# Rewritten order of work in the input stage of a decoder block: passes grouped by part, one product moved between plain halves, squares, diagonals and rotary tables moved

## The chip, the cores and the metric

The kernel runs on one core of one Trainium2 chip. The metric is the device time of one execution in microseconds. Everything is in fp32 at the borders; the kernel is a single program in which most engines' instructions stand in the order in which the program writes them.

## What is computed

One decoder block for 1024 tokens with 1024 features, all fp32:

```python
h = rms_norm(x, mix_norm_g)
z_a, q, k, v, gate_logits = split(h @ w_in)           # z_a = (u, v) of the gMLP, 2 x 768
# A: chunks of 128 tokens, 4 channel groups, causal weights w_spatial
u, v = split(gelu(z_a));  v = rms_norm(v, gmlp_norm_g)
mixed = einsum('gts,bcsgd->bctgd', tril(w_spatial), v_chunks) + b_spatial
y_a = u * mixed
# B: dilated sliding-window attention, 12 heads of 64, rotary on the first quarter
q, k = partial_rope(q, positions), partial_rope(k, positions)
y_b = dilated_mixture_attention(q, k, v)
merged = sigmoid(g_A) * (y_a @ w_branch_a) + sigmoid(g_B) * (y_b @ w_branch_b)
x = x + merged @ w_out
h2 = rms_norm(x, ffn_norm_g)
a, val = split(h2 @ w_up)                             # 2 x 2816
x = x + (gelu(causal_dwconv3(a)) * val) @ w_down
return rms_norm(x, final_norm_g)
```

## The kernel before

**How a product is made.** Each fp32 operand of a large product is split into two parts, a high part (the value rounded to the short form `fp32r`) and a low part (the rest). A product is then three passes of matmuls: high weight by high left, high weight by low left, low weight by high left. `PASSES` lists them as pairs (w, a): w is the part of the weight, which is loaded into TensorE and stays, and a the part of the left side, which streams through. ScalarE (ACT) makes every high part by a copy, VectorE (DVE) every low part by subtracting that copy. For weights that is lines 165 and 166 (`to_parts`), for the left quarters lines 405, 406, 411 and 412 (`in_left`; where the part is wanted negated the copy scales by -1).

**The two ways of the input projection.** The columns of `w_in` are worked through in pairs n of two blocks of 128. Pairs 0 and 1, the first 512 columns of v, are plain products (`plain_op`, `plain_step`, `plain_final`): each covers two halves h of 512 tokens and two blocks i, with 8 k-tiles and so 24 matmuls of 128x512 for each (n, h, i). Their left side is x times the gain alone (`raw_left`), and the factor of the RMS norm comes in later, so TensorE can work before the norm is known. From pair 2 (`FIRST`) on, each pair takes the seven products of Strassen's scheme in Winograd's form, in the order P1, P2, P6, P7, P5, P4, P3 for pair 2 and P1, P6, P2, P7, P5, P4, P3 behind it. Each is a call of `in_product` and has 4 k-tiles, so 12 matmuls of 128x512. Their left sides are quarters of the normed x or sums of quarters (`LEFT`): P1 takes A11, P2 A12, P6 S2, P7 S3, P5 S1, P4 A22, P3 S4. P2, P4 and P3 add into the PSUM banks of P1, P7 and P5 (`SHARED`). After a product, ACT or DVE takes its bank: P1's is copied by ACT (line 530), P6, P7, P5, P4 and P3 are added by DVE into the result (line 537 is P7's), and for the gMLP's columns ACT then runs gelu.

**From the plain pairs to the normed x.** `beginning()` writes this order out. `square_row` (line 366) squares rows of x on ACT with a sum, four for each half; `load_rows` fetches the rows. `root` (GpSimd, POOL) makes the inverse root. `diagonal` (lines 383 and 385) puts the factors on four 128x128 diagonals, for half 0 on DVE and for half 1 on ACT. `spread` (line 391) multiplies them by a matrix of ones on TensorE, and `scale_x` (line 456) multiplies x by gain and spread factor on DVE, in place, one call for each k-tile. `x_sum` and `x_sum_dma` (line 474, an accumulating DMA of POOL's queue) form the sums of quarters, `parts_of` the two parts of each quarter. `in_load` fetches a weight block on SP's queue, and `in_ahead(i, far, look)` loads weight blocks up to `far` products ahead and makes the parts of those up to `look` ahead.

**What sets the order.** From the start up to product number `ORDERED` = 6 of the Strassen list (P3 of pair 2), DVE and ACT execute in exactly the written order (a manual schedule); behind that a scheduler places DVE's and ACT's work. TensorE's matmuls run in the written order throughout. `meanwhile(i)` is called after the i-th product and writes the preparations of later ones: S3 after P1, S1 after P2, A22 after P6, S4 after P7. Each product gives two ticks of a clock, one after each six matmuls, and `after(t, fn)` runs `fn` t ticks later. By these ticks `turn_v` (line 623) transposes blocks of v, with ACT taking the bank by a gelu into V (line 628); `norm_v` squares a row block of V (ACT, line 192), takes the root and scales (DVE, line 640); `spatial` (lines 652 and 660, bank `pm`) multiplies it by the causal weights, with DVE taking the bank. `turn_v`, `spatial`, `spread` and the rotary transposes share the two PSUM banks with the tag `tr`.

**The rotary tables.** `rot_tables` returns three lists: some 40 small steps of DVE and ACT that lead to the sines, sixteen widening copies on ACT (line 2238), and four turns, each of four transposes on TensorE (line 2255) and a copy by ACT (line 2256). `some(n)` writes the next n steps. Before, what is left of the steps and all widening copies come at `i == 6`, and all four turns at `i == 8`.

**The up stage.** Near 800 us the products with `w_up` begin (`beginning_up`). `up_product` is built like `in_product`, with its banks taken by DVE, and `up_ahead(load, op)` loads weight blocks and makes their high parts, up to those two numbers. Here DVE's low parts are not written at once: they go to a list, and `low(n)` writes the next n of them. `first_taps` is the first part of a convolution, four DVE operations.

## Time and profile before

| | |
|---|---|
| median of 3 runs | 1389.06 us (1388.65 to 1392.38) |
| profiled execution, its time | 1391.06 us |
| profiled execution, its span in the trace | 1389.1 us |
| mean granted TensorE clock in it | 0.996 |
| instructions in the span | 19247 |
| HBM traffic | 167.77 MB read, 64.29 MB written, 167 GB/s over the span |

The profile is one execution as the hardware profiler recorded it. A page gives for each engine (PE is TensorE's matmuls, PEld its weight loads, DVE VectorE, ACT ScalarE, POOL GpSimd, SP SyncE) its busy time and its share of the span. Views of the trace list waits (an engine, its line, what it waited for, the total, the number and the largest), a timeline of one engine (start, length, line, instruction, output<-inputs, sizes, count; in brackets the idle time before it and what ended it), and stretches of time with the busy time of each engine and the clock that was granted to TensorE. All times are in us from the span's start. The median of the runs lies 2.00 below the profiled execution's time.

### The profile page before, as it was taken

The numbers are of one execution on the slowest core, as the hardware profiler recorded it, in microseconds if no ns is written. First come the engines' busy times: TensorE is split into PE (matmuls) and PEld (weight loads), VectorE is DVE, ScalarE is ACT, GpSimd is POOL, SyncE is SP. The second block draws the span as 40 slices with busy tenths as digits, with TensorE's granted clock in tenths as the row PEclk, the third lists the DMA queues.
The fourth block names the chain that finished last, engine by engine and source line by source line (L and its number), as shares of the span: only waits on it lengthen the run. The fifth ranks groups of instructions, "written<-read, shape, count | busy, mean of one in ns | idle before, by whom it ended". The sixth has DMA issues, their size and how long they took to land.

```text
span 1389.1 us, 19247 instructions
## 1 busy us (share of the span) xinstructions
PE 1364.6 (98%) x6434; PEld 1130.7 (81%) x6434; DVE 1030.6 (74%) x1880; ACT 655.1 (47%) x1289; POOL 298.1 (21%) x295
## 2 busy tenths in 40 slices
PE   9889999999999999999999999999999999999997
PEld 7767888888888888888788878888888888888886
DVE  7868677686877987867889887766766667676674
ACT  7583355555544333634646444333433335455443
POOL 0111000000221000120001146655566553000003
PEclk9999999999999999999999999999999999999999
DMA  9424535354435997694843133333323327986563
GB/s 352 89 65 130 167 109 169 115 167 134 130 116 193 329 307 256 216 300 140 287 133 104 39 117 103 106 107 113 107 103 110 122 84 254 385 322 221 196 206 122
DMA packets 143875, 237.01 MB, mean 171 GB/s; under 512 B 13728, under 2 KB 57504, under 8 KB 143776
## 3 DMA queue, kind: packets, MB, share of 16 engines
q1 hardware_dynamic: 141248, 231.53, 49.5%
q0 software_dynamic: 1088, 2.10, 0.9%
q10 hardware_dynamic: 1440, 2.16, 0.4%
q8 instruction: 51, 0.84, 0.2%
q14 instruction: 48, 0.39, 0.1%
HBM read 167.77 MB, written 64.29 MB: 167 GB/s over the span
## 4 chain that ended last, share of the span: by engine, by line
PE 85%; DVE 6%; ACT 3%; issue 2%; POOL 2%; DMA 2%; SPq 0%; POOLq 0%; ACTq 0%; DVEq 0%
PE in_P L510 25%; PE uP L1788 19%; PE dn L2046 13%; PE up L1788 8%; PE pa L1260 5%; PE wo_P L1621 4%; PE pl L571 2%; PE pu L1767 2%; PE pb L1260 1%; PE pu L851 1%; DMA ld<-scr 1%; PE pp L835 1%; DVE G L166 1%; PE pm L660 1%; POOL st L903 1%
## 5 line engine op out<-in xcount | busy, mean ns | idle before, releaser
L510 PE MATMUL in_P<-R,G 128*128 128x512 f32 x1008 | 243.8, 394 | 1.8 <-ACT C L530 1.8
L510 PEld LDWEIGHTS in_P<-R,G 128*128 128x128 f32 x1008 | 185.4, 188 | 38.5 <-ACT C L530 2.2
L2046 PE MATMUL dn<-R 128*128 128x512 f32 x924 | 209.6, 389 | 0.0
L2046 PEld LDWEIGHTS dn<-R 128*128 128x128 f32 x924 | 173.4, 188 | 36.0
L165 ACT ACTIVATE G<-wr 128x512 fp32r<-128x512 f32 x126 | 79.1, 630 | 150.4 <-PE in_P L510 114.4
L165 ACT ACTIVATE R<-up 128x512 fp32r<-128x512 f32 x130 | 78.8, 627 | 125.1 <-DVE up L278 40.9
L510 PE MATMUL in_P<-G,G 128*128 128x512 f32 x504 | 124.1, 397 | 2.3 <-DVE C L537 2.3
L1788 PE MATMUL up<-G,R 128*128 128x512 f32 x504 | 121.4, 391 | 1.7 <-DVE R L166 1.7
L1788 PE MATMUL uP<-G,R 128*128 128x512 f32 x504 | 121.2, 389 | 0.0
L1788 PE MATMUL uP<-R 128*128 128x512 f32 x504 | 121.1, 389 | 0.0
L1788 PEld LDWEIGHTS up<-G,R 128*128 128x128 f32 x504 | 94.5, 188 | 22.7 <-DVE R L166 2.2
L510 PEld LDWEIGHTS in_P<-G,G 128*128 128x128 f32 x504 | 93.7, 190 | 21.1 <-ACT G L405 2.5
L1788 PEld LDWEIGHTS uP<-G,R 128*128 128x128 f32 x504 | 94.5, 188 | 19.8 <-issue 0.2
L1788 PEld LDWEIGHTS uP<-R 128*128 128x128 f32 x504 | 94.6, 188 | 19.6
L166 DVE TENSOR_TENSOR G<-wr,G 128x512 fp32r<-128x512 f32 x126 | 87.9, 699 | 24.2 <-ACT G L165 24.0
L166 POOL TENSOR_TENSOR R<-up,R 128x512 fp32r<-128x512 f32 x55 | 84.0, 1527 | 74.5 <-ACT R L165 74.5
L166 DVE TENSOR_TENSOR R<-up,R 128x512 fp32r<-128x512 f32 x75 | 63.0, 841 | 16.1 <-ACT R L165 15.9
L165 ACT ACTIVATE R<-db 128x512 fp32r<-128x512 f32 x77 | 48.1, 626 | 56.3 <-PE dn L2046 45.3
L166 DVE TENSOR_TENSOR R<-db,R 128x512 fp32r<-128x512 f32 x77 | 53.7, 701 | 25.8 <-ACT R L165 25.7
L1260 PE MATMUL pa<-R,G 128*128 128x512 f32 x288 | 67.9, 389 | 0.0
L1260 PEld LDWEIGHTS pa<-R,G 128*128 128x128 f32 x288 | 54.1, 188 | 11.2
L510 PE MATMUL in_P<-G 128*128 128x512 f32 x252 | 62.2, 393 | 0.0
(279 smaller groups left out, 2396.5 us busy)
## 6 DMA issues: line engine op xcount, KB each, us to landing
wr<-in_w_in_dram SPq DMA_DIRECT2D x45, 512.0 KB, 4.1
up<-in_w_up_dram SPq DMA_DIRECT2D x44, 512.0 KB, 3.5
dA<-gd SPq DMA_DIRECT2D x55, 256.0 KB, 5.1
wd<-in_w_down_dram SPq DMA_DIRECT2D x44, 256.0 KB, 5.5
wT<-wd SPq DMA_DIRECT2D x44, 256.0 KB, 3.7
dS<-gS SPq DMA_DIRECT2D x44, 256.0 KB, 4.2
db<-wT SPq DMA_DIRECT2D x44, 256.0 KB, 4.2
gd<-Y SPq DMA_DIRECT2D x42, 256.0 KB, 2.0
```

Of the source, the lines that this page charges most:

```text
L165: nc.scalar.activation(hi, src, AF.Copy)
L166: fn = lambda: lo_eng.tensor_tensor(lo, src, f32(hi), ALU.subtract)
L510: nc.tensor.matmul(acc, op[:, w, kt, :], left[LEFT[name], kt][:, a, :], start=opened and kt == 0 and i == 0, stop=kt == QK - 1 and i == 2, ...
L571: nc.tensor.matmul(acc, plain_ops[n, k, i][:, w, kt, :], raw_x[h, k * QK + kt][:, a, :], start=k == 0 and kt == 0 and p == 0, stop=k == 1 ...
L660: nc.tensor.matmul(pm[:, o : o + P], v[:, c * P : (c + 1) * P], wspT[:, c * 2 // 3, :], start=True, stop=True,)
L835: nc.tensor.transpose(pp[:, i * P : (i + 1) * P], self.pr[:, h, s * P : (s + 1) * P], ident)
L851: nc.tensor.matmul(pu[:, h * HD : (h + 1) * HD], self.pT[:, i, :], vt[:, h * HD : (h + 1) * HD], start=i % n == 0, stop=i % n == n - 1,)
L1260: nc.tensor.matmul(acc, unit[a][kt // 4][:, kt % 4, :], two(R, 8 * h + kt)[:, b, :], start=n == 0 and i == 0, stop=n == len(kts) - 1 and i ...
L1621: nc.tensor.matmul(acc, left[LEFT[name], kt][:, a, blk * P : (blk + 1) * P], out_ops[s][:, w, :], start=name not in SHARED and kt == 0 and ...
L1767: nc.tensor.matmul(acc, plain_up[which, k][:, w, kt, :], left[f"A{h + 1}{k + 1}", kt][:, a, :], start=n == 0 and i == 0, stop=n == KT - 1 ...
L1788: nc.tensor.matmul(acc, op[:, w, kt, :], left[LEFT[name], kt][:, a, :], start=opened and kt == 0 and i == 0, stop=kt == QK - 1 and i == 2, ...
L2046: nc.tensor.matmul(accs[blk], dops[s][:, 0, a, blk * P : (blk + 1) * P], dops[s][:, 1, w, :], start=SEQ[j] not in CONTINUES and kt == 0 an ...
```

## The change

TensorE does the same matmuls. What changes is their order inside a Strassen product, and where several steps are written:

- Within `in_product` and `up_product`, the order was by k-tile, with the three passes for each. Now (`HIGH_FIRST`) all four high by high matmuls come first, then the four with the low part of the weight, then the four with the low part of the left. Ticks stay after six and after twelve.
- The rows of half 0 are fetched ahead of one weight block; the squares of half 0, its root and its diagonal are written ahead of the weight parts of pair 1; the first spread comes after the first k-tile of the second half of product (0, 1, 1) (before: after the third).
- The second diagonal is written between the first two and the last two parts of A11, and the second spread after the first k-tile of the product (1, 0, 1).
- A22's four high parts are written already ahead of the product (1, 1, 0), their low parts after product number 3.
- P1 of pair 2 stands between the two halves of the last plain product (1, 1, 1).
- S3 and S1 are both written after product 0, S4 after product 4; the transposes of the first v blocks start three ticks after that.
- The written order reaches to product number 9. What is left of the rotary steps and the widening copies are written there, and the turns, two each, after products 11 and 12. The turns take a bank of another pool instead of the two `tr` banks.
- In the up stage, weight parts up to 18 are made, and two low parts written, ahead of `first_taps(2)`, where it was up to 17 and one.

```diff
@@ -158,6 +158,9 @@
     PASSES = ((0, 0), (0, 1), (1, 0))
 
 
+    HIGH_FIRST = [(w, a, kt) for w, a in ((0, 0), (1, 0), (0, 1)) for kt in range(D // P // 2)]
+
+
     waiting = []
     written = [False]
 
@@ -303,7 +306,7 @@
 
 
     FIRST = 2
-    ORDERED = 6
+    ORDERED = 9
     in_order = [(FIRST, name) for name in ("P1", "P2", "P6", "P7", "P5", "P4", "P3")]
     for n in range(FIRST + 1, NP_IN):
         in_order += [(n, name) for name in ("P1", "P6", "P2", "P7", "P5", "P4", "P3")]
@@ -345,8 +348,8 @@
         load_x(0, range(k * QK, (k + 1) * QK))
     in_load(0, 1)
     load_x(1, range(KT))
+    load_rows(0)
     in_load(1, 0)
-    load_rows(0)
     in_load(1, 1)
 
     nc.vector.memset(mhalf, -0.5)
@@ -505,15 +508,14 @@
             acc = ps_d.tile([P, HALF], F32, name=f"in_{n}_{name}", tag="dn")
         in_banks[n, name] = acc
         op = in_ops.pop((n, name))
-        for kt in range(QK):
-            for i, (w, a) in enumerate(PASSES):
-                nc.tensor.matmul(
-                    acc, op[:, w, kt, :], left[LEFT[name], kt][:, a, :],
-                    start=opened and kt == 0 and i == 0,
-                    stop=kt == QK - 1 and i == 2,
-                    skip_group_check=not opened,
-                )
-            if kt % 2 == 1:
+        for i, (w, a, kt) in enumerate(HIGH_FIRST):
+            nc.tensor.matmul(
+                acc, op[:, w, kt, :], left[LEFT[name], kt][:, a, :],
+                start=opened and i == 0,
+                stop=i == len(HIGH_FIRST) - 1,
+                skip_group_check=not opened,
+            )
+            if i % 6 == 5:
                 tick()
         kind, _ = PAIRS[n]
         func = FUNC.get(kind, AF.Copy)
@@ -1045,11 +1047,19 @@
     ps_x_stack = ExitStack()
     wd_step = 0
 
+    rot_halves = []
+
+    def rot_bank(name):
+        if not rot_halves:
+            t = ps_x.tile([P, 2, HALF], F32, name=name, tag="sc")
+            rot_halves.extend((t[:, 1], t[:, 0]))
+        return rot_halves.pop()
+
     def beginning():
 
         chain, wide, turns = rot_tables(
             nc, lent, [[YC[:, i, lower], YC[:, i, upper]] for i in range(2)],
-            tr_tile, ident, positions, YC,
+            rot_bank, ident, positions, YC,
         )
         chain = iter(chain)
 
@@ -1089,31 +1099,38 @@
             raw_parts(1, kt)
         product(0, 1, 0)
         plain_final(0, 0, 1)
-        weight(1, 0, 0)
-        weight(1, 1, 0)
         for b in range(4):
             square_row(0, b)
         load_rows(1)
         root(0)
-        some(14)
+        some(16)
         diagonal(0)
+        weight(1, 0, 0)
+        weight(1, 1, 0)
         plain_final(0, 1, 0)
         weight(1, 0, 1)
         weight(1, 1, 1)
         product(0, 1, 1, (0,))
         for kt in range(QK):
             plain_step(0, 1, 1, 1, kt)
-            if kt == 2:
+            if kt == 0:
                 bc0 = spread(0)
         for kt in range(KT):
             scale_x(0, kt, bc0)
-        plain_final(0, 1, 1)
         for b in range(4):
             square_row(1, b)
         root(1)
-        parts_of("A11")
+        a11 = [in_left("A11", kt, quarter(0, 0, kt)) for kt in range(QK)]
+        for hi, lo in a11[:2]:
+            hi()
+            lo()
+        diagonal(1)
+        for hi, lo in a11[2:]:
+            hi()
+            lo()
+        plain_final(0, 1, 1)
         product(1, 0, 0)
-        diagonal(1)
+        plain_step(1, 0, 1, 0, 0)
         bc1 = spread(1)
         for kt in range(QK):
             scale_x(1, kt, bc1)
@@ -1122,33 +1139,40 @@
             if kt % 2 == 1:
                 x_sum_dma(3, kt // 2)
         plain_final(1, 0, 0)
-        product(1, 0, 1)
+        for n in range(1, KT):
+            plain_step(1, 0, 1, n // QK, n % QK)
         plain_final(1, 0, 1)
         parts_of("A12")
+        a22 = [in_left("A22", kt, quarter(1, 1, kt)) for kt in range(QK)]
         in_ahead(0, 9, 2)
+        for hi, _ in a22:
+            hi()
         product(1, 1, 0)
         plain_final(1, 1, 0)
         for kt in range(2):
             x_sum(2, kt)
         parts_of("S2", range(2))
-        product(1, 1, 1)
+        product(1, 1, 1, (0,))
         in_ahead(0, 9, 3)
+        in_product(FIRST, "P1")
+        product(1, 1, 1, (1,))
         for kt in range(2, QK):
             x_sum(2, kt)
         parts_of("S2", range(2, QK))
         plain_final(1, 1, 1)
         for k in range(2):
             x_sum_dma(4, k)
-        return some, wide, turns
+        return some, wide, turns, a22
 
     def meanwhile(i):
         if i == 0:
             parts_of("S3")
-        elif i == 1:
+            in_ahead(1, 9, 4)
             parts_of("S1")
-        elif i == 2:
-            parts_of("A22")
         elif i == 3:
+            for _, lo in a22:
+                lo()
+        elif i == 4:
             parts_of("S4")
             x_stack.close()
             zv["pool"] = zv_stack.enter_context(
@@ -1156,27 +1180,28 @@
             )
             open_zv()
             for b in range(0, NB, 2):
-                after(1 + b // 2, lambda b=b: turn_v(1, C[1], b))
-                after(5 + b // 2, lambda b=b: turn_v(0, C[0], b))
-        elif i == ORDERED:
+                after(3 + b // 2, lambda b=b: turn_v(1, C[1], b))
+                after(7 + b // 2, lambda b=b: turn_v(0, C[0], b))
+        elif i == 9:
             some(99)
             for fn in wide:
                 fn()
-        elif i == ORDERED + 2:
-            for fn in turns:
-                fn()
+        elif i in (11, 12):
+            turns.pop(0)()
+            turns.pop(0)()
 
     ordered = ExitStack()
     ordered.enter_context(
         tc.manual_schedule(engines={mybir.EngineType.DVE, mybir.EngineType.Activation})
     )
-    some, wide, turns = beginning()
+    some, wide, turns, a22 = beginning()
     for i, (n, name) in enumerate(in_order):
         in_ahead(i, 9, 4 if i else 2)
         if PAIRS[n][0] == "zu" and name == "P1":
             for c in range(2 * PAIRS[n][1], 2 * PAIRS[n][1] + 2):
                 nc.sync.dma_start(ya[:, c, :], mixd[c])
-        in_product(n, name)
+        if i:
+            in_product(n, name)
         meanwhile(i)
         if i == ORDERED:
             ordered.close()
@@ -1783,15 +1808,14 @@
             acc = banks[ff, SHARED[name]]
         banks[ff, name] = acc
         op = ops.pop((ff, name))
-        for kt in range(QK):
-            for i, (w, a) in enumerate(PASSES):
-                nc.tensor.matmul(
-                    acc, op[:, w, kt, :], left[LEFT[name], kt][:, a, :],
-                    start=opened and kt == 0 and i == 0,
-                    stop=kt == QK - 1 and i == 2,
-                    skip_group_check=not opened,
-                )
-            if kt % 2 == 1:
+        for i, (w, a, kt) in enumerate(HIGH_FIRST):
+            nc.tensor.matmul(
+                acc, op[:, w, kt, :], left[LEFT[name], kt][:, a, :],
+                start=opened and i == 0,
+                stop=i == len(HIGH_FIRST) - 1,
+                skip_group_check=not opened,
+            )
+            if i % 6 == 5:
                 tick()
         u2, v, c21, c12 = u2s[ff % 2], vs_[ff % 2], c21s[ff % 2], c12s[ff % 2]
         ge0, ge1 = ge_of(ff, 0), ge_of(ff, 1)
@@ -1969,8 +1993,8 @@
         up_product(2, "P7")
         up_ahead(18, 16)
         up_product(2, "P5")
-        up_ahead(18, 17)
-        low(1)
+        up_ahead(20, 18)
+        low(2)
         first_taps(2)
         up_product(2, "P4", lambda: up_ahead(20, 19))
         low(1)
```

## The prediction

> **What bounds the kernel now.** I read the busy shares first, then TensorE's waits, then its timeline over the first 130 us with the granted clock, then what VectorE and ScalarE were doing at each wait.
>
> ```profile
> PE 1364.6 (98%) x6434; PEld 1130.7 (81%) x6434; DVE 1030.6 (74%) x1880; ACT 655.1 (47%) x1289; POOL 298.1 (21%) x295
> ...
> PE in_P L510 <- DVE C L537: 2.3, 1, 2.3
> PE in_P L510 <- ACT C L530: 1.8, 1, 1.8
> PE rs_bc L391 <- ACT C L385: 1.8, 1, 1.8
> PE up L1788 <- DVE R L166: 1.7, 1, 1.7
> ...
> PE rot L2255 <- ACT YC L2256: 1.4, 1, 1.4
> ...
> PE vt L623 <- ACT V L628: 1.3, 1, 1.3
> PE rot L2255 <- ACT YC L2238: 1.1, 1, 1.1
> ```
>
> TensorE (PE) is busy 98% of the span, with as many weight loads as matmuls, so only its waits can be won. All of these but the `up` one lie in the input stage. They understate what is lost there, because matmuls that run late or at a lower clock count as busy. So I compare the stage with its content. In the timeline (start, length, instruction, count):
>
> ```profile
> 24.77 2.88 PE L571 MATMUL pl<-G 128*128 128x512 f32 x12
> 27.49 2.20 PE L571 MATMUL pl<-R,G 128*128 128x512 f32 x9
> 29.53 1.05 PE L391 MATMUL rs_bc<-C,ones 128*128 128x128 f32 x8
> 30.34 6.40 PE L571 MATMUL pl<-R,G 128*128 128x512 f32 x27
> ...
> 75.14 1.96 PE L510 MATMUL in_P<-G,G 128*128 128x512 f32 x6 [2.33 <-DVE C L537]
> 78.38 1.12 PE L623 MATMUL vt<-ident,C 128*128 128x128 f32 x4 [1.28 <-ACT V L628]
> ...
> 84.27 0.60 PE L623 MATMUL vt<-ident,C 128*128 128x128 f32 x4
> 84.62 1.64 PE L510 MATMUL in_P<-G 128*128 128x512 f32 x6
> ...
> 96.03 1.45 PE L2255 MATMUL rot<-ident,YC 128*128 128x128 f32 x8 [1.13 <-ACT YC L2238]
> 98.90 1.14 PE L2255 MATMUL rot<-ident,YC 128*128 128x128 f32 x8 [1.42 <-ACT YC L2256]
> ...
> 108.08 0.38 PE L660 MATMUL pm<-wspT,V 128*128 128x128 f32 x2
> 110.02 3.00 PE L510 MATMUL in_P<-G,G 128*128 128x512 f32 x12
> 119.56 3.00 PE L510 MATMUL in_P<-R,G 128*128 128x512 f32 x12
> ```
>
> Twelve matmuls take 27.49-24.77 = 2.72 us, 0.227 each; a spread takes 0.81 (29.53 to 30.34), a transposing unit `vt` 0.35, a spatial unit `pm` 1.94, a `rot` turn about 0.4. From 24.77 to the first product of pair 4 at 119.56 there are 288 wide matmuls (65.3), two spreads (1.6), 12 `vt` (4.3), four `rot` (1.6) and three `pm` (5.8): 78.6 us of content in 94.8. So 16.2 us are lost, more than the waits show, partly because of the clock (columns: stretch, its length, PE busy and instructions, granted clock, DMA share, GB/s):
>
> ```profile
> 76.20:76.40 0.20, 0.20 (x2) 0.58 0.49 184
> 83.00:83.20 0.20, 0.20 (x2) 0.85 0.33 80
> 1383.00:1384.00 1.00, 0.00 (x0) 0.77 0.88 334
> ```
>
> After the gap of 2.33 us the granted clock falls to half at 76.3 and returns at 83.1, 6.8 us later; after PE's end it falls again. That one drop cost half of the 5.5 us in which PE worked in it, 2.7.
>
> **The change, part by part.** Written order is what the engines execute here, so I followed the new queues of PE, DVE and ACT instruction by instruction, each with the duration of its row:
>
> ```profile
> 24.64 1.06 ACT L366 ACTIVATE YC<-YC 128x1024 f32<-128x1024 f32 x1 [1.39 <-DMA YC<-in_x_dram]
> 72.57 2.17 ACT L405 ACTIVATE G<-X 128x512 fp32r<-128x512 f32 x4
> 77.49 1.57 ACT L628 ACTIVATE V<-vt,rs_x 128x256 f32<-128x256 f32 x4 [2.23 <-DVE G L406]
> 95.09 3.28 ACT L2238 ACTIVATE YC<-ones 128x128 f32<-128x128 f32 x16
> 100.70 0.84 ACT L192 ACTIVATE junk_v<-V 128x768 bf16<-128x768 f32 x1
> 101.67 0.84 ACT L192 ACTIVATE junk_v<-V 128x768 bf16<-128x768 f32 x1
> ...
> 30.62 5.36 DVE L456 SCALAR_TENSOR_TENSOR X<-X,chan,rs_bc 128x512 f32<-128x512 f32 x8 [0.20 <-PE rs_bc L391]
> 39.90 1.41 DVE L456 SCALAR_TENSOR_TENSOR X<-X,chan,rs_bc 128x512 f32<-128x512 f32 x2 [0.78 <-PE rs_bc L391]
> 48.08 2.49 DVE L406 SCALAR_TENSOR_TENSOR R<-X,R 128x512 fp32r<-128x512 f32 x4
> 71.30 2.49 DVE L412 TENSOR_TENSOR G<-X,G 128x512 fp32r<-128x512 f32 x4
> 73.71 0.68 DVE L166 TENSOR_TENSOR G<-wr,G 128x512 fp32r<-128x512 f32 x1
> ```
>
> A high copy costs 0.52 on ACT, a low part or sum 0.60 on DVE (71.30 to 73.71 for four), a V square 0.97.
>
> *Rows, squares, first diagonal.* The rows go ahead of one 512 KB load in SP's queue and the squares ahead of two high copies (1.1), so I put the third row's landing, 24.6 before, at 23.6 and the diagonal at 27.8; the spread then goes out after 15 of 24 matmuls, at 28.2, without a wait. All four weight lows now stand ahead of the first scaling on DVE, so it begins at 30.4 against 30.6: worth nothing. A row one microsecond later than that moves everything up to the V copies by one.
>
> *Second diagonal.* It stands after two of the A11 high copies. Squares end near 32.5, the diagonal at 35.5, and PE comes to the spread at 37.1: its wait of 1.8 goes. DVE's second scaling starts at 38.2 instead of 39.9.
>
> *P1 between the plain halves.* P2 no longer follows P1 in the same bank; twelve plain matmuls (2.7) hide ACT's copy of it, and 1.8 goes. The copy ends near 55.9, P2 starts at 56.3; a DVE queue 0.5 later would bring the wait back.
>
> *High products first.* A low part of the left is needed 8 matmuls (1.8) into a product, that of the weights four (0.9). Nothing is added: as many matmuls, loads and ticks.
>
> *What is late next.* DVE. From 38.2 it has 8.2 of scaling and sums (39.90 to 48.08), then 33 operations (20.0) and 2.6 of waits on ACT and on itself up to the P7 sum, which ends at 69.0. P4 adds into P7's bank and cannot start before, while P5 ends at 67.2: 1.8 lost, as A22's low parts stand behind that sum. Four low parts of A22, one of pair 3 and the P5 sum follow, to 72.6. ACT's gelu of that sum stands ahead of S4's high copies, so the first is ready at 73.8; P4 has ended at 71.7: 2.1 lost, and 0.9 more as copies at 0.52 feed matmuls at 0.23. Behind S4's lows DVE forms pair 3's sums (2.2), and ACT has that high copy, the gelu of P4's sum and one more high copy ahead of the first V copy, which ends at 82.3. There are two `tr` banks, so the third `vt` waits for it from 78.2 to 82.4: 4.2 lost.
>
> *Tables last.* P1, P6 and P2 of pair 3 with nine `vt` end at 94.1, P7 and P5 at 99.6, `pm` 0 at 101.5. The first `rot` wants four of the sixteen widening copies (0.2 each), and ACT has ahead of them V squares 5 and 6 and a high copy that waits on a DVE sum behind P5's: P5's sum 102.4, that sum 103.3, copy and squares 2.6, widening 0.8: 106.8. Lost: 5.3, and 0.4 before the second turn; before it was 1.1 and 1.4.
>
> Lost in all: 1.8+3.0+4.2+5.7 = 14.7 against 16.2 (1.5 less; pair 4 at 118.1), before any clock drop. No row shows the clock in the new gaps. Below, it does not drop: 0. Above, the two gaps of 4.2 and 5.3 cause a drop each, as 2.33 and 1.28 did, and half clock lasts for 1.7 to 5.1 us of work after each restart, 0.85 to 2.55 lost apiece. I take 1.7 apiece, 3.4, since both gaps are longer than the one that did it.
>
> The Trainium skill, "TensorE: Matmul & The Clock Gate", section on the HAM clock gate, says that PE is dropped to half clock after an idle window of about 3.4 us and released after a busy one; both new gaps exceed that, so by its rule each would cost about 1.7 here, as I take. The old drop followed a gap of only 2.33, so the trace is stricter than the page.
>
> *The sums by DMA on POOL.*
>
> ```profile
> 44.40 1.42 POOL L474 DMA_DIRECT2D X<-X  x1 [6.94 <-DVE YC L463]
> 61.05 1.22 POOL L474 DMA_DIRECT2D X<-X  x1 [4.12 <-DMA X<-X]
> ```
>
> Four of these go one after another, 5.5 apart; starting at 42.5 the last lands near 63.5. S4 is read at 73: hidden by DVE's queue, with 9 us to spare.
>
> *The up stage.*
>
> ```profile
> 814.36 0.61 PE L1788 MATMUL up<-G,R 128*128 128x512 f32 x2
> 816.71 2.57 PE L1788 MATMUL up<-G,R 128*128 128x512 f32 x10 [1.74 <-DVE R L166]
> ...
> 815.98 0.68 DVE L166 TENSOR_TENSOR R<-up,R 128x512 fp32r<-128x512 f32 x1
> ```
>
> The third matmul starts 1.9 late, for a low part at 815.98. It now stands ahead of the taps, at about 809.7, and is wanted two matmuls later. DVE's taps move back by 0.7, with the next low part at 817.8 for a matmul at 818.0. Between 0 and -1.9: I take -1.7.
>
> Sum: -1.5 + 3.4 - 1.7 = +0.2. The profiled execution took 1391.06 for a span of 1389.1; its changed twin would take 1391.3. The median is 2.0 lower: 1389.06 + 0.2 = **1389.3**.
>
> **Rivals.**
>
> *The clock stays up.* For it: the waits of 1.1 and 1.4 near 97 caused no drop. Against: they were short. 0.2 - 3.4: 1385.9.
>
> *The chain on DVE is shorter than I add up.* If P3 and the third `vt` do not wait (3.0 and 4.2), one clock drop goes too: 0.2 - 7.2 - 1.7 = -8.7, 1380.4. For it: every wait of mine rests on a queue of some forty DVE rows. Against: those durations hardly vary.
>
> *Slower: the late tables push back the V squares.* Square 7 now stands behind the widening copies, its scaling on DVE (111.9) ahead of `pm` 1's eviction, done at 115.0; `pm` 2 wants those banks at 116.2. With ACT over 1.2 later than I have it, PE waits there too, one for one. With a third drop (1.7) and 3 us of waits: +4.9, 1394.0. For it: before, all eight squares ran without a table load between them. Against: the margin.
>
> *The up edit only moves the wait to the next product*: +1.9, 1391.0.
>
> **How the numbers follow.** Forecast 0.38 (its own range 1386 to 1393), clock up 0.13, shorter DVE chain 0.24, late squares 0.20, up edit void 0.05. The range: below, the second rival; above, both clock drops at their dearest (5.1), no gain in up and a wait at `pm`: +3.6 and 2.3, so 1380 to 1395. A change under 0.3% (4.2 us) can't be told from none. Faster than 1384.9: the shorter chain and half of the clock's case, 0.30; slower than 1393.2: the late squares and a little of the forecast, 0.22; within: 0.48.
>
> **What would show it.** Right: no wait before the second spread and P2; PE waiting for the P7 sum, for S4's copies, before the third `vt` and before the first `rot` near 101; half clock after each of the last two; no wait near 815. Wrong: V copies starting before 78, a `rot` without a wait, a full clock throughout, or new waits at `pm`.

## The result, and the profile after

The changed kernel takes 1396.31 us (median of 7 runs, 1395.07 to 1398.77) beside 1392.38 for the kernel before (7 runs, 1388.65 to 1393.70): a ratio of 1.0036, 95% interval 1.0022 to 1.0050. The ratio is that of the means, which are 5.0 apart; the medians are 3.9 apart. It is slower, by 3 to 7 us, where 1389.3 and no measurable difference were forecast. The forecast was added to a median of three runs, 1389.06; the seven runs have 1392.38, so 3.3 of the 7.0 between 1389.3 and 1396.31 are in that base and not in the change. The profiled execution has a span of 1395.6, 6.5 more than the one before.

The waits of TensorE (engine, line, what it waited for, total, number, longest), changed kernel:

```profile
PE vt L625 <- ACT V L630: 3.8, 1, 3.8
PE rot L2279 <- ACT YC L2262: 3.7, 1, 3.7
PE rot L2279 <- ACT YC L2280: 2.8, 2, 1.8
PE in_P L512 <- DVE C L539: 2.7, 2, 1.7
PE in_P L512 <- ACT G L408: 1.7, 1, 1.7
...
PE up L1812 <- ACT t L1825: 1.5, 1, 1.5
PE uP L1812 <- DVE R L169: 0.9, 1, 0.9
```

The waits for the second diagonal and for P1's bank (1.8 each) are gone, as the change wants. In their place stand those that the prediction listed, and others that it did not have, or not in this size: the third row, turns that wait for the copy of another turn (it has 0.4 for that), and the last two, in the up stage. Of the two waits in the fourth row, one (1.0) lies far behind, at 497.09. TensorE's timeline shows where they lie (start, length, instruction, count, idle time before and its end):

```profile
28.17 1.05 PE L394 MATMUL rs_bc<-C,ones 128*128 128x128 f32 x8
...
37.25 1.05 PE L394 MATMUL rs_bc<-C,ones 128*128 128x128 f32 x8
...
64.70 2.88 PE L512 MATMUL in_P<-G,G 128*128 128x512 f32 x12
69.26 2.98 PE L512 MATMUL in_P<-G,G 128*128 128x512 f32 x12 [1.68 <-DVE C L539]
73.95 2.53 PE L512 MATMUL in_P<-G 128*128 128x512 f32 x6 [1.71 <-ACT G L408]
...
82.51 1.11 PE L625 MATMUL vt<-ident,C 128*128 128x128 f32 x4 [3.76 <-ACT V L630]
83.28 2.91 PE L512 MATMUL in_P<-R,G 128*128 128x512 f32 x6
...
104.99 0.49 PE L662 MATMUL pm<-wspT,V 128*128 128x128 f32 x2
109.21 1.12 PE L2279 MATMUL rot<-ident,YC 128*128 128x128 f32 x4 [3.73 <-ACT YC L2262]
112.07 1.12 PE L2279 MATMUL rot<-ident,YC 128*128 128x128 f32 x4 [1.75 <-ACT YC L2280]
112.84 4.10 PE L512 MATMUL in_P<-G,G 128*128 128x512 f32 x12
...
118.80 0.60 PE L2279 MATMUL rot<-ident,YC 128*128 128x128 f32 x4
120.43 0.66 PE L2279 MATMUL rot<-ident,YC 128*128 128x128 f32 x4 [1.03 <-ACT YC L2280]
...
125.62 3.00 PE L512 MATMUL in_P<-R,G 128*128 128x512 f32 x12
```

P5 of pair 2 starts at 64.70 where it started at 69.02: the early part of the change wins 4.3. Pair 4 starts at 125.62 where it started at 119.56: between the two 10.4 are given back. From there to the up stage (P1 of its block 4, 814.36 before and 819.85 after) 0.6 is won: three waits of the kernel before between 406 and 672 (1.7 in all) don't appear again, and the one of 1.0 at 497.09 is new. The up stage costs 0.9 more: 6.06 - 0.57 + 0.91 = 6.4 of the 6.5.

The granted clock, in stretches of 3.41 us that end where it changes (stretch, length, PE, PEld, DVE, ACT and POOL busy, granted clock, DMA share, GB/s):

```profile
70.84:74.25 3.41, 1.70 (x8) 1.01 (x6) 2.19 (x5) 1.50 (x3) 0.00 (x0) 1.00 0.24 95
77.67:81.08 3.41, 1.08 (x7) 0.68 (x5) 2.07 (x4) 1.13 (x2) 0.00 (x0) 1.00 0.17 44
81.08:84.49 3.41, 1.98 (x7) 1.79 (x8) 1.29 (x2) 2.93 (x8) 0.00 (x0) 0.50 0.20 54
84.49:87.91 3.42, 3.42 (x13) 2.93 (x13) 2.07 (x3) 1.64 (x4) 0.55 (x3) 0.50 0.32 94
104.97:108.38 3.41, 0.51 (x4) 0.30 (x2) 3.41 (x14) 2.84 (x9) 1.22 (x3) 1.00 0.00 0
```

The clock is at half from 81.1 to 87.9 and from 108.4 to 115.2, once after each of the two long gaps, as forecast. The last row also shows that VectorE works without a pause while TensorE waits for the tables.

### The profile page after: what moved, and what is told of

It reads as the page before. It is cut to its first block, busy times and chain, and to the rows that moved or that the text cites. A ratio compares the mean times of both kernels' runs of the same rounds, so it can differ in the third digit from the quotient of the medians.

```text
span 1395.6 us, 19216 instructions
## 1 busy us (share of the span) xinstructions
PE 1367.8 (98%) x6434; PEld 1132.7 (81%) x6434; DVE 1030.4 (74%) x1880; ACT 653.7 (47%) x1289; POOL 299.2 (21%) x295
## 5 line engine op out<-in xcount | busy, mean ns | idle before, releaser
L169 DVE TENSOR_TENSOR G<-wr,G 128x512 fp32r<-128x512 f32 x126 | 87.9, 698 | 32.9 <-ACT G L168 31.9
L168 ACT ACTIVATE R<-db 128x512 fp32r<-128x512 f32 x77 | 48.1, 625 | 56.4 <-PE dn L2070 45.6
```

What stands on the lines that cost most here:

```text
L168: nc.scalar.activation(hi, src, AF.Copy)
L169: fn = lambda: lo_eng.tensor_tensor(lo, src, f32(hi), ALU.subtract)
```

## The experiments

The kernels differ in when their first rows land (up to 0.8 us), so I measure the input stage inside each run, from the first matmul of P4 of pair 2 to the first product of pair 4: 56.4 in the changed kernel (69.26 to 125.62). The table has that distance, the lengths of the stretches at half clock in the input stage of the profile, the median, and the ratio to the kernel before on the same chip.

| kernel | P4 to pair 4 | half clock | median | ratio, 95% interval |
|---|---|---|---|---|
| changed | 56.4 | 6.8, 6.8 | 1396.31 | 1.0036, 1.0022 to 1.0050 |
| up_by_ktile | 55.6 | 3.4, 6.8 | 1395.24 | 1.0024, 1.0014 to 1.0034 |
| up_edit_undone | 55.5 | 3.4, 6.8 | 1395.32 | 1.0036, 1.0022 to 1.0051 |
| rot_two_tiles | 51.5 | 3.4, 6.8 | 1392.81 | 1.0017, 1.0004 to 1.0029 |
| fill_gaps | 54.0 | 3.4 | 1394.30 | 1.0029, 1.0018 to 1.0040 |
| chain_early | 50.1 | 6.8 | 1389.27 | 0.9992, 0.9982 to 1.0001 |
| tables_old_place | 56.6 | 3.4, 6.8, 3.4 | 1397.11 | 1.0048, 1.0030 to 1.0066 |
| vt_later | 52.2 | 3.4, 3.4, 6.8 | 1393.91 | 1.0022, 1.0009 to 1.0036 |
| all_mended | 42.5 | none | 1384.40 | 0.9959, 0.9946 to 0.9972 |
| tables_mended | 46.3 | 3.4, 3.4 | 1384.96 | 0.9956, 0.9943 to 0.9969 |
| rewritten | 41.4 | none | 1380.18 | 0.9919, 0.9906 to 0.9933 |
| high_only (on the kernel before) | other order | 6.8, 3.4 | 1391.16 | 1.0001, 0.9992 to 1.0011 |

### The order of passes alone

```diff
 kernel before
+    HIGH_FIRST = [(w, a, kt) for w, a in ((0, 0), (1, 0), (0, 1)) for kt in range(D // P // 2)]
     in in_product and in up_product:
-        for kt in range(QK):
-            for i, (w, a) in enumerate(PASSES):
+        for i, (w, a, kt) in enumerate(HIGH_FIRST):
```

> The kernel before with one part of the change alone: in all Strassen products of the input and the up stage the four high by high matmuls first, then the low part of the weight, then the low part of the left. Theory: the order of the passes alone does next to nothing in the input stage, whose waits are for sums, copies and diagonals: pair 4 starts within 0.5 us of 119.56. In the up stage the low part near 816 is wanted two matmuls later, so its wait of 1.7 shrinks to 1.3, and the span is 0 to 0.5 us shorter than 1389.1. Rival: the order by itself brings the later waits of the up stage (1.5 and 0.9), and the span is 0.5 to 1.5 us longer.

The run does not differ from the kernel before. In the up stage the wait for the low part is 1.1 instead of 1.7. The input stage missed its mark, pair 4 at 121.28 and not within 0.5 of 119.56: the waits are the same up to 94, but the scheduler put a copy into V ahead of the turns' copies, one wait of 2.2 came of it, and the clock fell a second time, for 3.4 us. Pair 4 is 1.7 late by that, and the up stage begins 0.1 late (814.46): the three waits between 406 and 672 are absent here too, and why is not shown. So the order by itself is worth about 0.6 in the up stage, and nothing that can be measured in the whole run.

### The up stage

```diff
 up_by_ktile: both; up_edit_undone: the second hunk only
-        for i, (w, a, kt) in enumerate(HIGH_FIRST):
+        for kt in range(QK):
+            for i, (w, a) in enumerate(PASSES):
 ...
-        up_ahead(20, 18)
-        low(2)
+        up_ahead(18, 17)
+        low(1)
```

> The changed kernel with the up stage written as before (order by k-tile, weight parts up to 17 and one low part ahead of the taps); the input stage stays changed. Theory: the up stage gave away about 1.0 us (from 5.5 behind the kernel before ahead of it to 6.5 behind it afterwards), because the shorter wait near 820 lets two later ones appear, 1.5 for the copy of P1's bank and 0.9 for a low part. Then the first product of pair 4 still starts at 125.6, the wait of 1.7 for a low part is back, the two others are gone, and the span is 1.0 us shorter than the changed kernel's 1395.6, so near 1394.6. Rival: those two waits come from the shift of everything before and not from the order; then they stay and the span is 1.7 longer, near 1397.

> The changed kernel with the up stage's passes high first, but weight parts up to 17 and one low part ahead of the taps as before. Theory: the edit of these two lines costs 1.6 (the order alone won 0.6 there, both together lost 1.0): the wait for a low part is back at 1.1, the two waits of 1.5 and 0.9 are gone, and from the first product of the up stage that waits to the end the run is 1.6 shorter than the changed kernel. Rival: the two waits belong to the order of passes together with the new arrival times; then they stay.

Both theories held in the profile for the up stage. (The span of up_by_ktile, 1393.7, is 0.9 below the one expected, since pair 4 starts at 124.42 and not at 125.6.) From the first matmul of P1 of block 4 to that of P2 of block 5 it takes 29.37 before (814.36 to 843.73), 29.34 with all undone (819.07 to 848.41), 30.28 in the changed kernel and 28.73 with the two lines undone. TensorE in the changed kernel, then in up_edit_undone:

```profile
819.85 2.88 PE L1812 MATMUL up<-G,R 128*128 128x512 f32 x12
...
829.71 3.00 PE L1812 MATMUL up<-G,R 128*128 128x512 f32 x12 [1.49 <-ACT t L1825]
...
845.42 2.11 PE L1812 MATMUL uP<-R 128*128 128x512 f32 x8 [0.93 <-DVE R L169]
...
850.13 2.25 PE L1812 MATMUL up<-G,R 128*128 128x512 f32 x9
```

```profile
819.32 1.07 PE L1812 MATMUL up<-G,R 128*128 128x512 f32 x4
821.49 2.11 PE L1812 MATMUL up<-G,R 128*128 128x512 f32 x8 [1.10 <-DVE R L169]
...
848.05 2.25 PE L1812 MATMUL up<-G,R 128*128 128x512 f32 x9
```

The order wins 0.6 and the two moved lines lose 1.5. Why is in ScalarE's rows. Two of the kernel before, then those of the changed kernel with VectorE's low part:

```profile
809.56 0.76 ACT L1721 ACTIVATE Y<-up,chan 128x512 f32<-128x512 f32 x1
...
822.30 0.58 ACT L1801 ACTIVATE t<-up 128x512 f32<-128x512 f32 x1
```

```profile
815.47 0.71 DVE L169 TENSOR_TENSOR R<-up,R 128x512 fp32r<-128x512 f32 x1 [1.22 <-ACT R L168]
...
816.29 0.78 ACT L1746 ACTIVATE Y<-up,chan 128x512 f32<-128x512 f32 x1 [0.85 <-DVE edge L1780]
...
828.02 0.63 ACT L1743 ACTIVATE Y<-Y 128x512 f32<-128x512 f32 x1 [1.66 <-DVE Y L1750]
...
829.08 0.58 ACT L1825 ACTIVATE t<-up 128x512 f32<-128x512 f32 x1
```

The taps go back and forth between VectorE and ScalarE. They started at 809.56 before, 815.0 with the 5.5 of delay that TensorE had by then; they start at 816.29, 1.2 later, since VectorE first waits 1.2 for a high copy of ScalarE and makes one low part (0.7); the other of the two weight parts has its low part on GpSimd (815.58). ScalarE's copy of block 4's P1 (done by TensorE at 822.6) stands behind the taps and comes at 829.08 (822.30 before, so 1.3 later too), and P2 of this block, which adds into the same bank, waits for it (829.71). P7 of block 4 then waits for its weight's low part, behind the next taps (845.42). In the medians the gain of up_edit_undone (1395.32 beside 1396.31) is within what the runs scatter, and the ratios are the same.

### The turns' tile

```diff
     def rot_bank(name):
-        if not rot_halves:
-            t = ps_x.tile([P, 2, HALF], F32, name=name, tag="sc")
-            rot_halves.extend((t[:, 1], t[:, 0]))
-        return rot_halves.pop()
+        rot_halves.append(name)
+        if len(rot_halves) % 2:
+            return ps_x.tile([P, 2, HALF], F32, name=name, tag="sc")[:, 0]
+        return ps_x.tile([P, HALF], F32, name=name, tag="pu")
```

> The changed kernel with the four rotary turns in two PSUM tiles by turns instead of the two halves of one tile. Theory: a turn waits for the copy of the turn before it only because both write one tile; with two tiles the second turn follows the first by 0.4 to 1.0 us instead of 2.9, the fourth the third by 0.4 instead of 1.6, and the first product of pair 4 starts 2.5 to 3.5 us earlier than 125.6; the span shrinks by as much. Rival: the second turn waits for the widening copies, or ScalarE's queue, whatever the tile; then it starts at 112 as before and nothing changes.

TensorE of this run:

```profile
106.32 1.97 PE L2279 MATMUL rot<-ident,YC 128*128 128x128 f32 x8 [3.78 <-ACT YC L2262]
...
114.80 1.04 PE L2279 MATMUL rot<-ident,YC 128*128 128x128 f32 x8
```

Two turns now run as one group of eight, with no wait inside, while the wait before the first (3.78) is as it was. So the second and the fourth turn had waited for a copy that reads the other half of their own tile: the wait belongs to the tile, not to the data. Of the 4.8 that the distance shrank, 2.1 and 1.2 are these waits; the rest, 1.5, I put down to the clock, whose first stretch was 3.4 long here and lay elsewhere; no run separates it.

### The clock

```diff
+    def fill(name, n):
+        t = acc_tile(name)
+        for _ in range(n):
+            nc.tensor.matmul(t[:, :P], ident, ident, start=True, stop=True)
 ...
+        if (p, b) == (2, 4):
+            fill(f"fill_{b}", 18)
         pt = tr_tile(f"vt_{p}_{b}")
 ...
         elif i in (11, 12):
+            if i == 11:
+                fill("fill_rot", 18)
             turns.pop(0)()
```

> The changed kernel with 18 extra 128x128 matmuls of the identity on TensorE into a PSUM bank that nobody reads, once ahead of the third transposing unit (the gap of 4.0 us at 78.5) and once ahead of the first rotary turn (the gap of 4.0 us at 105.2). Theory: the granted clock falls because TensorE stands idle in them; filled, it stays at 1.00 from 70 to 125, the two stretches of 6.8 us at half clock are gone, and the first product of pair 4 starts 3.5 to 4.6 us earlier (2.7 of the work after the first gap, 1.9 after the second, less what a wait on ScalarE gives back), near 121.5. Rival: the clock falls for another reason than idleness, or what follows is set by VectorE and ScalarE anyway: then pair 4 starts within 1 us of 125.6.

The stretches of this run that hold the filled gaps (columns as above):

```profile
79.97:83.39 3.42, 3.42 (x32) 3.42 (x31) 2.11 (x4) 2.57 (x6) 0.00 (x0) 1.00 0.51 55
...
103.87:107.28 3.41, 3.41 (x32) 3.14 (x31) 3.41 (x13) 2.83 (x7) 1.14 (x4) 1.00 0.00 0
```

The clock did not fall after either filled gap, while it fell after both in each of the three runs with the same input stage (changed, up_by_ktile, up_edit_undone). It did fall earlier, at 76.6 for 3.4 us, where P3 is fed by S4's copies. The extra matmuls ran longer than the gap and made the first product of pair 3 1.3 later (15.3 behind P4, 14.0 in the changed kernel); from there to pair 4 it takes 38.8 instead of 42.3. So the half clock had cost 3.6 behind that point, and the total gain of 2.3 is short of the 3.5 to 4.6 expected, for which I give that overrun and the earlier fall.

### The tables

```diff
 chain_early
+        elif i == 7:
+            some(15)
         elif i == 9:
             some(99)

 tables_old_place
-    ORDERED = 9
+    ORDERED = 6
-        elif i == 9:
+        elif i == 6:
             some(99)
 ...
-        elif i in (11, 12):
-            turns.pop(0)()
-            turns.pop(0)()
+        elif i == 8:
+            for fn in turns:
+                fn()
     and tr_tile in the place of rot_bank
```

> The changed kernel with one edit: the fifteen remaining VectorE steps of the rotary tables are written after product 7 (P1 of pair 3), where VectorE stands idle from 87.5 to 92.2, instead of after product 9; sines, widening copies and turns stay. Measured from the first matmul of P4 of pair 2 (69.26 in the changed kernel) the first product of pair 4 starts 56.4 later there. Theory: the first turn waits for this chain of small steps (the last at 106.7, the sines at 107.2, widening from 108.3); with the steps done by 94 the sines follow the last gelu of V near 99, widening ends near 105, the first turn waits 0.5 or less instead of 4.0, the second half-clock stretch is gone, and the 56.4 become 49.5 to 51.5. Rival: ScalarE's queue (table load, squares) or the steps' new place ahead of weight parts sets the turn; then it gains 1 or less, 55 to 57.

The theory held, at 50.1. ScalarE and then TensorE of this run:

```profile
97.90 0.83 ACT L630 ACTIVATE V<-vt,rs_x 128x256 f32<-128x256 f32 x2
...
99.22 1.28 ACT L2258 ACT_TABLE_LOAD   x1
100.52 0.26 ACT L2258 ACTIVATE ones<-ones 128x64 f32<-128x64 f32 x1
100.68 0.24 ACT L2259 ACTIVATE ones<-ones 128x64 f32<-128x64 f32 x1
...
101.66 3.28 ACT L2264 ACTIVATE YC<-ones 128x128 f32<-128x128 f32 x16
```

```profile
104.95 0.60 PE L2281 MATMUL rot<-ident,YC 128*128 128x128 f32 x4
106.82 0.66 PE L2281 MATMUL rot<-ident,YC 128*128 128x128 f32 x4 [1.27 <-ACT YC L2282]
```

Fifteen small VectorE steps, written two products earlier into VectorE's idle time, let the sines follow the last gelu of V; the first turn waits for nothing and the second stretch at half clock is gone. This one edit takes 5 to 7 us off the changed kernel and brings it level with the one before.

> The changed kernel with the tables back where the kernel before has them: remaining steps and widening after product 6, the four turns after product 8 in the two banks of the transposing units, written order up to product 6; everything else stays changed. Theory: what the late tables cost is not cured by the old place, because the copies into V now come later and stand behind the sines: ScalarE loads the sine table, waits for VectorE's steps (from 83 to 87), and must load the gelu table again for V, so the transposing units wait 4 to 6 more near 85, while the turns no longer wait. From P4 of pair 2 to pair 4 it takes 52 to 55 (56.4 in the changed kernel, 50.1 with the early steps). Rival: the old place alone takes back the whole loss of the tables, the turns and the second stretch at half clock: 47 to 50.

The direction of the theory held, the size did not: 56.6, worse than 52 to 55. Two transposing units, at 84.42 and 95.03, wait 8.0 together, the clock is at half for 13.7 us in all, and the turns wait 1.2. ScalarE:

```profile
86.70 1.28 ACT L2256 ACT_TABLE_LOAD   x1
88.45 0.26 ACT L2256 ACTIVATE ones<-ones 128x64 f32<-128x64 f32 x1 [0.46 <-DVE ones L2217]
89.40 0.26 ACT L2257 ACTIVATE ones<-ones 128x64 f32<-128x64 f32 x1 [0.69 <-DVE ones L2217]
89.67 1.28 ACT L630 ACT_TABLE_LOAD   x1
```

The sines stand between two gelus of V and cost two table loads; before, they came after the last gelu. So the old place is no cure under the new early part, and "tables last" was not wrong as such: the steps that lead to them were too late.

### The transposing units, and all of it together

```diff
 vt_later, and in all_mended
-                after(3 + b // 2, lambda b=b: turn_v(1, C[1], b))
-                after(7 + b // 2, lambda b=b: turn_v(0, C[0], b))
+                after(5 + b // 2, lambda b=b: turn_v(1, C[1], b))
+                after(9 + b // 2, lambda b=b: turn_v(0, C[0], b))
     and two ticks more for pair 2's units, the squares and the spatial units
```

Written that late, pair 1's last transposing units read a block into which P1 of pair 3 has already been copied, so these two kernels compute a wrong V; the number and the sizes of the instructions are the same. They serve for timing alone.

> The changed kernel with all transposing units, squares and spatial units of v two ticks (one product) later; tables and turns stay. Theory: the third transposing unit waits 4.0 for the first copy into V, which stands on ScalarE behind the sums of VectorE; one product later it waits 1.5 or less, TensorE stays more than half busy and the first half-clock stretch goes, so the first spatial unit comes 4 to 5 us earlier against P4 of pair 2 than in the changed kernel. The first turn then still waits for the tables, which hang on VectorE and ScalarE: of the 56.4 from P4 to pair 4 only 2 to 3 are won, 53.5 to 54.5. Rival: the tables move up with TensorE, and all 5 arrive: 51 to 52.

The distance is 52.2 with one spatial unit (1.9) fewer ahead of pair 4, so 54.2 like for like: the size that the theory gave, but not all of its mechanism. The third unit waits 2.1 where 1.5 or less was expected, and the clock still falls early, twice for 3.4. A turn waits 4.4: what the units no longer wait, the turns do.

> The changed kernel with the transposing units, squares and spatial units one product later, the VectorE steps of the tables after product 7, sines and widening after product 10, turns after products 12 and 13 in two PSUM tiles, and the up stage's weight parts and low parts as before (the passes stay high first). Theory: the early part of the change wins about 4 us by P5 of pair 2, and what it lost is in four places that each edit takes away: the first product of pair 4 then starts about 40 us after P4 of pair 2 with one spatial unit less ahead of it (42 with it, 56.4 in the changed kernel), no stretch at half clock or one of 3.4 us, and the run is near 1383, 8 to 9 us below the kernel before. Rival: the waits come back elsewhere, at the later squares of V or the spatial units, and the run is within 3 us of the kernel before.

42.5, 44.4 like for like (42 expected), no half clock, 1384.40: 6.5 below the kernel before in the medians, where 8 to 9 were expected. The third unit still waits 3.5 here, since the first copy into V stays behind other work of ScalarE; moving the units alone does not cure that.

> The changed kernel with three edits: the fifteen VectorE steps of the tables after product 7, the turns in two PSUM tiles, and the up stage's weight and low parts as before. Theory: the three costs are separate and add up. From P4 of pair 2 to the first product of pair 4 it takes 50.1 (measured with the early steps alone) less the two waits for copies of turns, 1.3 and 1.2: 46.5 to 48.5; the up stage takes 1.6 less; the run is near 1385.5, 5 to 6 us below the kernel before. Rival: the turns' waits only move to the spatial units, or the gains overlap, and the run is at 1387 to 1389.

46.3 and 1384.96: the three costs are separate and add up, within what the clock moves. The 46.3 lie 0.2 below the range; chain_early's 50.1 less its two waits for turns would be 47.7, and the clock was at half for 3.4 twice here instead of 6.8 at a stretch.

```diff
 rewritten = tables_mended and
+    LOOK = {0: 2, 2: 3, 3: 2, 4: 2, 5: 3, 6: 3}
-        in_ahead(i, 9, 4 if i else 2)
+        in_ahead(i, 9, LOOK.get(i, 4))
+        if i == 4:
+            for hi, _ in s4[2:]:
+                hi()
+            for _, lo in a22:
+                lo()
+            in_ahead(i, 9, 3)
 ...
         elif i == 3:
-            for _, lo in a22:
-                lo()
+            s4.extend(in_left("S4", kt, quarter(0, 1, kt)) for kt in range(QK))
+            for hi, _ in s4[:2]:
+                hi()
         elif i == 4:
-            parts_of("S4")
+            for _, lo in s4:
+                lo()
 ...
-                after(3 + b // 2, lambda b=b: turn_v(1, C[1], b))
-                after(7 + b // 2, lambda b=b: turn_v(0, C[0], b))
+                after((1, 2, 4, 5)[b // 2], lambda b=b: turn_v(1, C[1], b))
+                after(6 + b // 2, lambda b=b: turn_v(0, C[0], b))
```

> The three edits of tables_mended, and the queues of VectorE and ScalarE between P7 and P1 of pair 3 rewritten after what the waits of the changed kernel showed: the P7 sum ahead of the weight parts of P4, S4's high parts ahead of the gelu of P5's sum, weight parts of P6 and P2 of pair 3 later than the first copies into V, and the transposing units of pair 1 at ticks 1, 2, 4, 5. Theory: the waits of 1.8 (P4), 2.0 and 1.0 (P3) and 4.0 (third transposing unit) are waits for places in these two queues, not for VectorE's work as such; P4 waits 0.5 or less, P3 1.2 or less, the third unit 1.2 or less, TensorE stays above half busy and the clock at 1.00 throughout. From the first matmul of P5 of pair 2 (60.9 in the changed kernel, 50.5 before) the first product of pair 4 starts 41.5 to 44 later, and the run is near 1379. Rival: VectorE's work itself is the bound, the waits come back behind S4's low parts or at the spatial units, and the run stays at 1383 to 1386.

TensorE of this run:

```profile
64.61 2.88 PE L512 MATMUL in_P<-G,G 128*128 128x512 f32 x12
67.94 1.66 PE L512 MATMUL in_P<-G,G 128*128 128x512 f32 x6 [0.45 <-ACT G L168]
...
72.36 2.99 PE L512 MATMUL in_P<-G 128*128 128x512 f32 x12 [0.35 <-DVE C L541]
75.63 0.66 PE L625 MATMUL vt<-ident,C 128*128 128x128 f32 x4 [0.28 <-ACT V L630]
...
98.12 1.04 PE L2292 MATMUL rot<-ident,YC 128*128 128x128 f32 x8
...
109.34 3.00 PE L512 MATMUL in_P<-R,G 128*128 128x512 f32 x12
```

Counted from the end of the work before, P4, P3 and the third unit wait 0.6 each (0.5, 1.2 and 1.2 or less were expected), the clock never falls before the end of TensorE's work, and pair 4 starts 44.7 behind P5 (60.9 in the changed kernel, 50.5 before). That is 0.7 over the range I gave, and 1380.18 beside "near 1379". VectorE does the same work (1880 instructions, busy for 1029.8 beside 1030.4 in the changed kernel): the waits were for places in the queues. This kernel is 0.8% faster than the one before, ratio 0.9919 (0.9906 to 0.9933).

## Why the prediction was wrong

The sum was +0.2, and the two profiled spans differ by 6.5. (From the median of seven runs, 1392.38, the same sum would have given 1392.6 with a range up to 1398.3, which holds 1396.31; but the medians' 3.9 and the spans' 6.5 are both far from 0.2, so steps of the sum failed.) By its own steps:

- *Rows, squares, first diagonal; second diagonal; P1 between the plain halves*: right. Spreads at 28.17 and 37.25 (28.2, 37.1 forecast), P2 at 56.54 (56.3), neither waits.
- *What is late next*: right in place and size. Waits counted from the end of the work before: P4 1.8 (1.8 forecast), P3 2.0 and 1.0 for the copies (2.1 and 0.9), third unit 4.0 (4.2).
- *Tables last*: the first turn's wait is 4.0 (5.3 forecast), 1.3 too dear. **Wrong: "0.4 before the second turn".** It takes 2.5 from the end of the first turn to the second, and 1.2 from the third to the fourth where none was forecast. I took two halves of one tile for two banks that are independent; rot_two_tiles shows that they are not. Without the half clock in it that is 2.9 too little.
- *The clock*: the mechanism was right, both gaps brought a fall. **Too small: "I take 1.7 apiece, 3.4".** Half clock lasted 6.8 each time, and the work in it after the restart was slowed by 2.7 (82.5 to 87.9) and 2.0 (109.2 to 115.2): 4.7, near the upper bound of 5.1. How long a fall lasts hung on where the clock's grid lay: in up_by_ktile, with the same waits, the first lasted 3.4 and cost the 1.7 that I took.
- *The content of 78.6* leaves out what a change between wide matmuls and a transposing unit costs: six wide matmuls and their unit took 1.83 (76.67 to 78.50) against 1.71 worked out. The 16.2 lost before are a difference of measured times and contain it, my 14.7 are a sum of waits and don't: about 1.0 for the nine units in my walk of pair 3.
- Together: 2.9 + 1.3 + 1.0 - 1.3, and 0.3 that I can't place, are the 4.2 between the input stage's forecast (+1.9) and its measure (+6.1).
- *The up stage*: **wrong, "Between 0 and -1.9: I take -1.7"**; it was +0.9. I followed VectorE and one low part, and moved the taps back by its 0.7. They move back by 1.2, since VectorE also waits for the high copy of that part, and once moved they take ScalarE's copy of a P1 bank and a later low part with them. The bounds held no loss at all. The rival "the up edit only moves the wait to the next product", with a chance of 0.05, came nearest; the waits came back three and eight products on, at 1.5 and 0.9. With the 4.2, this step's 2.6 and the 0.6 won in between, the 6.3 between +0.2 and 6.5 are told but for 0.1.
- The rivals: the clock did not stay up; VectorE's chain was as long as added up; the spatial units waited for nothing, so the slower case that I named is not the one that came.

The largest error is thus a wait between halves of a tile and a queue (ScalarE in the up stage) that I did not follow; the range ended 1.3 below the measured 1396.31, less than the 3.3 by which the base was low. That the late tables were what lost the gain stood in the prediction, at 5.3 + 0.4 + 1.7; with the measured sizes and the up stage's sign the forecast would have been slower.

## What to carry to other kernels

A gain at the head of a stage is only a gain if what is due next in the queues moves up with it: the 4.3 won by P5 were lost behind instructions that kept their old neighbours, and came back when the queues of VectorE and ScalarE were written again after the waits. Small steps that lead to a late result belong into the idle time of their engine, far ahead of the result. Two halves of a tile were one tile for waits here (2.1 and 1.2 us), and an engine that only passes values on (here ScalarE in the taps) has to be followed like the one that is late.

## What the runs showed of the hardware

The granted clock falls and returns on a grid of 3.41 us whose position differs from run to run. In the changed kernel all four changes (81.08, 87.91, 108.39, 115.21) are whole steps of 3.41 apart; in up_by_ktile, with the same input stage, they lie at 83.46, 86.87, 107.35 and 114.18, and the first stretch is 3.4 instead of 6.8 long. With the same waits, pair 4 starts 0.8 earlier behind P4 there. The scatter of the kernel before goes with the clock too: of its 61 runs beside the experiments, the 27 with a mean granted clock of 0.997 or more average 1389.7, the other 34 1391.9.

A stretch need not be idle to bring the fall. Of the grid's stretches between 60 and 125 us in eleven of the profiles (all_mended and rewritten have no fall there to place the grid by), every one in which PE was busy for 0.43 or less of the time was followed by half clock (16 of them), every one at 0.70 or more by full clock, and those between went both ways, for instance 0.50 with full clock (70.84:74.25 above) and 0.48 with half (rot_two_tiles, 71.28 to 74.69). At half clock, stretches busy for 0.92 or more brought the full clock back (21 of 21), those up to 0.73 did not (10 of 10). So two waits of 1.7 us close together, as in rot_two_tiles, can bring the fall as one of 4 does. The Trainium skill, "TensorE: Matmul & The Clock Gate", section "The HAM clock gate", has the window of 3.4 us and its free position, which these runs agree with (3.41); its condition for the fall, an idle window, is narrower than what they show.
